# A hybrid decoder layer on one core: weights of every third MLP step combined on VectorE, one step in advance

## The chip, the cores and the metric

The kernel runs on one core of a Trainium2 chip. The core has a matrix engine (TensorE, called PE in the profile, with its weight loads as PEld), VectorE (DVE), ScalarE (ACT), GpSimd (POOL) and SyncE (SP), whose queue issues nearly all DMA transfers here. Each engine takes its instructions in order; engines wait for each other by semaphores. Tiles live in SBUF, a memory of 128 partitions; results of matmuls go to PSUM, eight banks of 128 x 512 float32.

The metric is the device time of one execution in microseconds (us), as a median over runs. A profile is one such execution with every instruction recorded.

## The reference, cut to what matters

One layer with 256 tokens and a width of 2048: a norm, one input projection, a state-space part and a sparse-attention part, an output projection into the residual, and then the MLP, which is the part that matters here:

```
u = rmsnorm(x, g_mlp) @ w_up                       # 256 x 2048 @ 2048 x 8192
return x + jnp.square(jax.nn.relu(u)) @ w_down     # 256 x 8192 @ 8192 x 2048
```

All is float32. The kernel reaches that precision by splitting each operand into a rounded part ("hi") and the rest ("lo"), both of a type that the matrix engine multiplies fast, and adding three products: hi x hi, lo x hi, hi x lo.

## The kernel before, in words

**Splitting weights.** Every weight goes the same way. SyncE's queue loads a block of 128 x 1024 float32 (512 KB) into a buffer called raw; ScalarE casts it to hi (line 144); VectorE subtracts hi from raw to get lo (line 145); hi and lo lie in one buffer, w2. There are RB = 4 raw buffers and WB = 5 w2 buffers. A raw buffer is free again when lo is made, a w2 buffer when the last matmul that reads it has run.

**The MLP.** The 8192 hidden columns are handled in pairs of 128-row blocks, 32 pairs, cut into three parts by `PARTS = (0, 11, 22, 32)`: 11, 11 and 10 pairs. For each part h, `up(h)` makes the hidden activations of all its pairs (line 230 holds the matmuls), and `down(h)` multiplies them with `w_down` and adds into the residual `xr`. The order on the profile's axis is up 0, down 0, up 1, down 1, up 2, down 2.

`down` runs over two halves j of the 2048 output columns. In each half it takes the pairs g in turn, a *step* each. A step has a 2 x 2 block of activations (two blocks of 128 tokens times two blocks of 128 hidden rows) and a 2 x 2 block of weights (two blocks of 128 hidden rows times two blocks of 512 columns). A plain step makes 8 products of blocks, each three matmuls of 512 columns in `three` (lines 189, 191, 192), so 24. The steps in `SEVEN = {2, 4, 6}` use seven products instead of eight (Winograd's form of Strassen's scheme), so 21 matmuls. For this, sums of the activations are made in `up` (lines 826 to 828), and sums of the weights in `weights` (lines 852 to 855): four subtractions of 128 x 512 on GpSimd, one after the other since three of them use the one before, one of them in place in raw. The results of the combination lie in raw[1] and in a tile t of 128 x 1536. Three casts (lines 860 and 863) and three subtractions (lines 861 and 864) split them into two w2 buffers and one buffer wt, of which there are two.

Four of the seven products are kept in accumulators of their own (p1, p5, p6, p7: four PSUM banks) over all three such steps of a half. After the last of these steps (`done`) they are combined on VectorE through two tiles s1 and s2 and added to the residual (lines 913 to 922). The other four banks hold the plain accumulators. The next half uses the two groups of four banks the other way round; so its plain products need the four banks of p1 to p7 from its first step on.

**What sets the order.** The matmuls run in the order in which the program states them. For the other engines and the DMA queues a planner orders the instructions at compile time by a model of their times: among those that are ready it takes the one with the highest priority, which is the order of the program, with all that stands under `tc.high_priority(offset=HP)` (loads and splits of weights) moved 600 instructions forward. On the chip each queue then keeps that order, and an instruction that has to wait holds up those behind it.

Of the kernel before, what the change touches and what calls it, by code (L numbers as in the profile page):

```python
# [9 lines left out]
F32 = mybir.dt.float32  # L10
# [3 lines left out]
OP = mybir.AluOpType  # L14
# [28 lines left out]
FIRST_W = 32  # L43


PARTS = (0, 11, 22, 32)
SEVEN = {2, 4, 6}

A11, A21, A12, A22 = range(4)
S3, S1, S2, S4 = 1, 4, 5, 6  # L50
# [34 lines left out]
def hymba_kernel(ctx: ExitStack, tc: tile.TileContext, xn, xt, w_in, w_out, w_up, w_down, vcol, vrow, out):  # L85
# [40 lines left out]
        return vc[:, VC[name] + i:VC[name] + i + 1]  # L126


    def operands(src, n, load=None, shift=0, parts=2):

        pitch = (n + 63) // 64 * 64
        with tc.high_priority(offset=HP):
            raw = wts.tile([P, parts, pitch], F32, name="raw", tag="raw", bufs=RB)
            both = wts.tile([P, 2 * parts * pitch + SPARE], F32R, name="w2", tag="w2", bufs=WB)
            hi, lo = (both[:, shift + i * parts * pitch:shift + (i + 1) * parts * pitch]
                      .rearrange("p (k c) -> p k c", k=parts)[:, :, :n] for i in range(2))
            src = src.rearrange("p (k c) -> p k c", k=parts)
            step = parts if load is None else 1
            for i in range(0, parts, step):
                s = slice(i, i + step)  # L140
                nc.sync.dma_start(raw[:, s, :n], src[:, s])
                if load is not None:
                    load()
                nc.scalar.copy(hi[:, s], raw[:, s, :n])  # L144
                nc.vector.tensor_tensor(lo[:, s], raw[:, s, :n], hi[:, s].bitcast(F32), op=OP.subtract)  # L145
        return hi, lo
# [663 lines left out]


    mlp = ctx.enter_context(tc.tile_pool(name="mlp", bufs=2))

    def up(h, tag):

# [18 lines left out]
            u.append((uh, ul))  # L834
        return u

    def weights(j, g, seven):


        if not seven:  # L840
            ops = [operands(w_down[2 * j + c, g], 512, shift=SHIFT) for c in range(2)]
            return [[(ops[c][0][:, k], ops[c][1][:, k]) for c in range(2)] for k in range(2)]
        with tc.high_priority(offset=HP):
            raws = []
            for c in range(2):
                raws.append(wts.tile([P, 2, 512], F32, name="raw", tag="raw", bufs=RB))
                nc.sync.dma_start(raws[c], w_down[2 * j + c, g].rearrange("p (k c) -> p k c", k=2))
            both = mlp.tile([P, 2 * 3 * 512 + SPARE], F32R, name="wt")
            th, tl = (both[:, SHIFT + i * 1536:SHIFT + (i + 1) * 1536].rearrange("p (k c) -> p k c", k=3) for i in range(2))
            t = mlp.tile([P, 3, 512], F32, name="t", bufs=1)  # L850

            nc.gpsimd.tensor_tensor(t[:, 0], raws[1][:, 1], raws[1][:, 0], op=OP.subtract)  # L852
            nc.gpsimd.tensor_tensor(raws[1][:, 0], raws[1][:, 0], raws[0][:, 0], op=OP.subtract)  # L853
            nc.gpsimd.tensor_tensor(t[:, 1], raws[1][:, 1], raws[1][:, 0], op=OP.subtract)  # L854
            nc.gpsimd.tensor_tensor(t[:, 2], raws[0][:, 1], t[:, 1], op=OP.subtract)  # L855
            ops = []
            for raw in raws:
                w2 = wts.tile([P, 2 * 2 * 512 + SPARE], F32R, name="w2", tag="w2", bufs=WB)
                hi, lo = (w2[:, SHIFT + i * 1024:SHIFT + (i + 1) * 1024].rearrange("p (k c) -> p k c", k=2) for i in range(2))
                nc.scalar.copy(hi, raw)  # L860
                nc.vector.tensor_tensor(lo, raw, hi.bitcast(F32), op=OP.subtract)  # L861
                ops.append((hi, lo))
            nc.scalar.copy(th, t)  # L863
            nc.vector.tensor_tensor(tl, t, th.bitcast(F32), op=OP.subtract)  # L864
        pick = lambda o, k: (o[0][:, k], o[1][:, k])
        (b11, b21), (t1, b22) = ([pick(o, k) for k in range(2)] for o in ops)
        t3, t2, t4 = (pick((th, tl), k) for k in range(3))
        return b11, b21, b22, t1, t2, t3, t4

    def down(h, u, tags):  # L870
        pairs = len(u)
        marked = SEVEN
        for j in range(2):
            end = h == 2 and j == 1
            outs = [accumulator(tags[j]) for _ in range(4)]
            acc = [outs[:2], outs[2:]]
            cut = CUTS if interrupted("down") else {}
            count = [0]

            def go(out, left, slot, w, first, last=False):  # L880
                three(out, left[0][:, slot], left[1][:, slot], *w, first, last, cut.get(count[0]))
                count[0] += 1

            def add(b, c, src, store=False):
                c = slice(1024 * j + c.start, 1024 * j + c.stop)
                nc.vector.scalar_tensor_tensor(xr[:, b, c], src, rs4[:, b:b + 1], xr[:, b, c], op0=OP.mult, op1=OP.add)
                if store:
                    nc.sync.dma_start(out[b * P:(b + 1) * P, c], xr[:, b, c])

            half = [slice(0, 512), slice(512, 1024)]  # L890
            ps7 = None
            kept = []
            for g in range(pairs):
                seven = g in marked
                w = weights(j, PARTS[h] + g, seven)
                if seven:
                    b11, b21, b22, t1, t2, t3, t4 = w
                    new = ps7 is None
                    if new:
                        ps7 = [accumulator(tags[1 - j]) for _ in range(4)]  # L900
                    p1, p5, p6, p7 = ps7
                    done = g == max(marked)
                    go(p1, u[g], A11, b11, new, done)
                    go(acc[0][0], u[g], A12, b21, False)
                    go(acc[0][1], u[g], S4, b22, False)
                    go(p5, u[g], S1, t1, new, done)
                    go(p7, u[g], S3, t3, new, done)
                    go(p6, u[g], S2, t2, new, done)
                    go(acc[1][0], u[g], A22, t4, False)
                    if done:  # L910

                        s1 = mlp.tile([P, 512], F32, name="s1", bufs=1)
                        nc.scalar.copy(s1, p1)
                        add(0, half[0], p1)
                        nc.vector.tensor_tensor(s1, s1, p6, op=OP.add)
                        s2 = mlp.tile([P, 512], F32, name="s2", bufs=1)
                        nc.vector.tensor_tensor(s2, s1, p7, op=OP.add)
                        add(1, half[0], s2)
                        nc.vector.tensor_tensor(s1, s1, p5, op=OP.add)
                        add(0, half[1], s1)  # L920
                        nc.vector.tensor_tensor(s2, s2, p5, op=OP.add)
                        add(1, half[1], s2)
                elif end and g >= pairs - 2:
                    kept.append((u[g], w))
                else:
                    for k in range(2):
                        for c in range(2):
                            for b in range(NB):
                                go(acc[b][c], u[g], 2 * k + b, w[k][c], g + k == 0, g == pairs - 1 and k == 1)
            if not end:  # L930
                for c in range(2):
                    for b in range(NB):
                        add(b, half[c], acc[b][c], h == 2)
                other.append("down")
                continue

            for b, c in ((0, 0), (1, 0), (0, 1)):
                for left, w in kept:
                    for k in range(2):
                        go(acc[b][c], left, 2 * k + b, w[k][c], False, left is u[-1] and k == 1)  # L940
                add(b, half[c], acc[b][c], True)
            c = slice(0, 256)
            for left, w in kept:
                for k in range(2):
                    go(acc[1][1][:, c], left, 2 * k + 1, [x[:, c] for x in w[k][1]], False, left is u[-1] and k == 1)
            add(1, slice(512, 768), acc[1][1][:, c], True)
            c = slice(256, 512)
            add(1, slice(768, 1024), acc[1][1][:, c])
            rest = accumulator(tags[0])[:, c]
            for i, (left, w) in enumerate(kept):  # L950
                for k in range(2):
                    go(rest, left, 2 * k + 1, [x[:, c] for x in w[k][1]], i + k == 0, left is u[-1] and k == 1)
            add(1, slice(768, 1024), rest, True)
# [56 lines left out]
```

## Time and profile before

| | |
|---|---|
| median of 3 runs | 1105.0 us (1101.55 to 1105.72) |
| the profiled execution | 1102.39 us, its span 1100.6 us |
| TensorE busy | 1070.3 us (97%) |
| VectorE, ScalarE, GpSimd busy | 746.4, 551.0, 123.5 us |
| mean granted clock of TensorE | 0.990 |
| bytes moved by DMA | 207.41 MB, mean 188 GB/s |

Rows of the profile name an engine, a line of the kernel, the tile written and, after the arrow, what was read (buffer numbers left out). In a row of waits, "A <- B: 15.6, 13, 1.3" says that A waited for B 15.6 us in all, in 13 places, 1.3 us at most. In a row of groups stand the count, the busy time, the mean duration in ns and the idle time before, with what ended it. In a table of stages each row has the stretch, its length, each engine's busy time with its number of instructions, the granted clock (1.00 is full speed), the DMA share and GB/s. Matmuls overlap in a pipeline: one of 512 columns is recorded with 0.38 us, while the next starts some 0.22 us after it.

### The profile page before, as it was taken

The numbers are of one execution on the slowest core, as the hardware profiler recorded it, in microseconds if no ns is written. First come the engines' busy times: TensorE is split into PE (matmuls) and PEld (weight loads), VectorE is DVE, ScalarE is ACT, GpSimd is POOL, SyncE is SP. The second block draws the span as 40 slices with busy tenths as digits, with TensorE's granted clock in tenths as the row PEclk, the third lists the DMA queues.
The fourth block names the chain that finished last, engine by engine and source line by source line (L and its number), as shares of the span: only waits on it lengthen the run. The fifth ranks groups of instructions, "written<-read, shape, count | busy, mean of one in ns | idle before, by whom it ended". The sixth has DMA issues, their size and how long they took to land.

```text
span 1100.6 us, 15648 instructions
## 1 busy us (share of the span) xinstructions
PE 1070.3 (97%) x5962; PEld 938.7 (85%) x5962; DVE 746.4 (68%) x1066; ACT 551.0 (50%) x749; POOL 123.5 (11%) x102
## 2 busy tenths in 40 slices
PE   9999999999999999999898999999998999998988
PEld 8999998888888898988686889897786888987876
DVE  6787997687665576764674767765665767754846
ACT  7755555567654554553544445544344445544433
POOL 0020000221000000003123000004123000023140
PEclk9999999999999999999999999999899999999999
DMA  9865437544565556664554766663554666645753
GB/s 329 261 213 182 158 105 241 172 135 135 165 236 187 187 185 201 196 197 150 186 178 161 242 207 195 194 207 134 192 186 169 226 202 192 198 147 172 239 163 115
DMA packets 63611, 207.41 MB, mean 188 GB/s; under 512 B 7088, under 2 KB 11440, under 8 KB 63536
## 3 DMA queue, kind: packets, MB, share of 16 engines
q1 hardware_dynamic: 63392, 206.36, 57.5%
q8 instruction: 47, 0.77, 0.3%
q14 instruction: 28, 0.23, 0.1%
q10 hardware_dynamic: 144, 0.05, 0.0%
HBM read 204.29 MB, written 2.10 MB: 188 GB/s over the span
## 4 chain that ended last, share of the span: by engine, by line
PE 73%; POOL 9%; DMA 5%; DVE 5%; issue 4%; ACT 4%; POOLq 0%; ACTq 0%; DVEq 0%
PE acc L230 29%; PE acc L192 10%; PE acc L209 10%; PE acc L189 10%; PE acc L191 10%; DMA raw<-in_w_down 5%; POOL raw L853 2%; DVE w L861 2%; POOL t L854 2%; POOL t L852 2%; POOL t L855 2%; ACT wt L863 2%; DVE w L145 2%; ACT w L144 2%; PE ps_y L610 1%
## 5 line engine op out<-in xcount | busy, mean ns | idle before, releaser
L145 DVE TENSOR_TENSOR w<-raw,w 128x1024 fp32r<-128x1024 f32 (+3 forms) x364 | 420.2, 1166 | 204.0 <-ACT w L144 203.1
L144 ACT CAST w<-raw 128x1024 fp32r<-128x1024 f32 (+3 forms) x364 | 357.5, 993 | 335.8 <-PE acc L192 104.7
L230 PE MATMUL acc<-x2x,w 128*128 128x512 f32 (+2 forms) x2053 | 343.0, 327 | 0.0
L230 PEld LDWEIGHTS acc<-x2x,w 128*128 128x128 f32 x2053 | 307.9, 188 | 34.4
L192 PE MATMUL acc<-w,uh 128*128 128x512 f32 (+1 forms) x444 | 171.9, 387 | 15.6 <-DVE w L861 15.6
L189 PE MATMUL acc<-w,uh 128*128 128x512 f32 (+5 forms) x459 | 171.4, 379 | 10.0 <-ACT w L860 10.0
L191 PE MATMUL acc<-w,ul 128*128 128x512 f32 (+1 forms) x444 | 169.4, 382 | 0.0
L209 PE MATMUL acc<-hx,w 128*128 128x256 f32 (+1 forms) x978 | 115.0, 277 | 0.0
L192 PEld LDWEIGHTS acc<-w,uh 128*128 128x128 f32 x444 | 83.7, 189 | 35.2 <-DVE w L861 21.0
L209 PEld LDWEIGHTS acc<-hx,w 128*128 128x128 f32 x978 | 112.7, 188 | 0.0
L189 PEld LDWEIGHTS acc<-w,uh 128*128 128x128 f32 x459 | 86.2, 188 | 29.2 <-ACT w L860 14.4
L864 DVE TENSOR_TENSOR wt<-t,wt 128x1536 fp32r<-128x1536 f32 x18 | 31.7, 1759 | 114.9 <-ACT wt L863 114.9
L852 POOL TENSOR_TENSOR t<-raw 128x512 f32<-128x512 f32 x18 | 24.7, 1373 | 716.5 <-DMA raw<-in_w_down 669.1
L191 PEld LDWEIGHTS acc<-w,ul 128*128 128x128 f32 x444 | 83.7, 188 | 14.4
L863 ACT CAST wt<-t 128x1536 fp32r<-128x1536 f32 x18 | 26.5, 1474 | 128.9 <-POOL t L855 128.9
L189 PE MATMUL acc<-w,hx 128*128 128x512 f32 (+3 forms) x228 | 83.9, 371 | 0.0
L191 PE MATMUL acc<-w,hx 128*128 128x512 f32 (+1 forms) x224 | 80.9, 361 | 0.0
L192 PE MATMUL acc<-w,hx 128*128 128x512 f32 (+1 forms) x224 | 80.7, 360 | 0.0
L189 PEld LDWEIGHTS acc<-w,hx 128*128 128x128 f32 x228 | 43.0, 189 | 6.1 <-issue 0.7
L191 PEld LDWEIGHTS acc<-w,hx 128*128 128x128 f32 x224 | 42.4, 189 | 5.9 <-issue 0.7
L192 PEld LDWEIGHTS acc<-w,hx 128*128 128x128 f32 x224 | 42.2, 189 | 6.0 <-DVE w L145 0.4
L861 DVE TENSOR_TENSOR w<-raw,w 128x1024 fp32r<-128x1024 f32 x36 | 46.1, 1279 | 0.2 <-ACT w L860 0.2
(229 smaller groups left out, 1033.3 us busy)
## 6 DMA issues: line engine op xcount, KB each, us to landing
raw<-in_w_up SPq DMA_DIRECT2D x128, 512.0 KB, 4.1
raw<-in_w_down SPq DMA_DIRECT2D x128, 512.0 KB, 4.3
raw<-in_w_in SPq DMA_DIRECT2D x72, 512.0 KB, 3.5
raw<-in_w_out SPq DMA_DIRECT2D x32, 512.0 KB, 3.3
raw<-in_w_in SPq DMA_DIRECT2D x16, 256.0 KB, 5.2
raw<-in_w_in SPq DMA_DIRECT2D x16, 152.0 KB, 5.2
raw<-in_w_in SPq DMA_DIRECT2D x8, 304.0 KB, 3.2
xT<-in_xt SPq DMA_DIRECT2D x8, 256.0 KB, 5.2
```

What stands on the lines that cost most here:

```text
L144: nc.scalar.copy(hi[:, s], raw[:, s, :n])
L145: nc.vector.tensor_tensor(lo[:, s], raw[:, s, :n], hi[:, s].bitcast(F32), op=OP.subtract)
L189: nc.tensor.matmul(go(out[:, i:j]), ah, go(wh[:, i:j]), start=first and i == 0, stop=False, skip_group_check=True)
L191: nc.tensor.matmul(go(out), al, go(wh), start=False, stop=False, skip_group_check=True)
L192: nc.tensor.matmul(go(out), ah, go(wl), start=False, stop=last, skip_group_check=True)
L209: nc.tensor.matmul(acc[:, c, at:at + n], w[:, 0, s], x[:, fr:fr + n], start=(i + k + j == 0), stop=(i >= 2 and k == 7 and j == len(todo) - ...
L230: nc.tensor.matmul(walk(out[:, at:at + n]), w[:, 0, s], walk(x[:, at:at + n]), start=(i < 2 and k + j == 0), stop=(i >= 2 and k == 7 and j ...
L852: nc.gpsimd.tensor_tensor(t[:, 0], raws[1][:, 1], raws[1][:, 0], op=OP.subtract)
L853: nc.gpsimd.tensor_tensor(raws[1][:, 0], raws[1][:, 0], raws[0][:, 0], op=OP.subtract)
L861: nc.vector.tensor_tensor(lo, raw, hi.bitcast(F32), op=OP.subtract)
L863: nc.scalar.copy(th, t)
L864: nc.vector.tensor_tensor(tl, t, th.bitcast(F32), op=OP.subtract)
```

## The change

- `PARTS` becomes (0, 10, 21, 32), so 10, 11 and 11 pairs, and `SEVEN` becomes {2, 5, 8}.
- While the MLP's pool exists, every second raw tile comes from it, under a tag with four buffers of its own: eight raw buffers from then on.
- `weights` is cut in three. `plain` is the old path of a plain step. `combine` loads the two raw tiles of a seven-product step and makes the four subtractions, now on VectorE; it is called one step earlier, ahead of the loads of the plain step before. `combined` makes the casts and rests, when the step itself comes.
- wt has one buffer instead of two, and s1 and s2 are taken from the two buffers of r (a tile that `up` uses) instead of having their own.

```diff
-PARTS = (0, 11, 22, 32)
-SEVEN = {2, 4, 6}
+PARTS = (0, 10, 21, 32)
+SEVEN = {2, 5, 8}
...
+    def raw_tile(parts, pitch):
+
+        taken[0] += 1
+        pool, tag = (mlp_pool[0], "rawm") if mlp_pool and taken[0] % 2 else (wts, "raw")
+        return pool.tile([P, parts, pitch], F32, name="raw", tag=tag, bufs=RB)
...
-            raw = wts.tile([P, parts, pitch], F32, name="raw", tag="raw", bufs=RB)
+            raw = raw_tile(parts, pitch)
...
+    def combine(j, g):
+
         with tc.high_priority(offset=HP):
             raws = []
             for c in range(2):
-                raws.append(wts.tile([P, 2, 512], F32, name="raw", tag="raw", bufs=RB))
+                raws.append(raw_tile(2, 512))
                 nc.sync.dma_start(raws[c], w_down[2 * j + c, g].rearrange("p (k c) -> p k c", k=2))
...
-            nc.gpsimd.tensor_tensor(t[:, 0], raws[1][:, 1], raws[1][:, 0], op=OP.subtract)
-            nc.gpsimd.tensor_tensor(raws[1][:, 0], raws[1][:, 0], raws[0][:, 0], op=OP.subtract)
-            nc.gpsimd.tensor_tensor(t[:, 1], raws[1][:, 1], raws[1][:, 0], op=OP.subtract)
-            nc.gpsimd.tensor_tensor(t[:, 2], raws[0][:, 1], t[:, 1], op=OP.subtract)
+            nc.vector.tensor_tensor(t[:, 0], raws[1][:, 1], raws[1][:, 0], op=OP.subtract)
+            nc.vector.tensor_tensor(raws[1][:, 0], raws[1][:, 0], raws[0][:, 0], op=OP.subtract)
+            nc.vector.tensor_tensor(t[:, 1], raws[1][:, 1], raws[1][:, 0], op=OP.subtract)
+            nc.vector.tensor_tensor(t[:, 2], raws[0][:, 1], t[:, 1], op=OP.subtract)
+        return raws[0], raws[1], t
+
+    def combined(raws):
+
+        ops = []
+        with tc.high_priority(offset=HP):
             for raw in raws:
-                w2 = wts.tile([P, 2 * 2 * 512 + SPARE], F32R, name="w2", tag="w2", bufs=WB)
...
+                n = raw.shape[1]
+                if n == 2:
+                    both = wts.tile([P, 2 * 2 * 512 + SPARE], F32R, name="w2", tag="w2", bufs=WB)
+                else:
+                    both = mlp.tile([P, 2 * 3 * 512 + SPARE], F32R, name="wt", bufs=1)
...
                 nc.scalar.copy(hi, raw)
                 nc.vector.tensor_tensor(lo, raw, hi.bitcast(F32), op=OP.subtract)
...
-                w = weights(j, PARTS[h] + g, seven)
+
+                if g + 1 in marked:
+                    ahead = combine(j, PARTS[h] + g + 1)
+                w = combined(ahead) if seven else plain(j, PARTS[h] + g)
...
-                        s1 = mlp.tile([P, 512], F32, name="s1", bufs=1)
+                        s1, s2 = (mlp.tile([P, 7, P], F32, name="r")[:, :4].rearrange("p k t -> p (k t)")
+                                  for _ in range(2))
...
-                        s2 = mlp.tile([P, 512], F32, name="s2", bufs=1)
```

More of the change, by code (lines that the diff above doesn't have):

```diff
@@ L126, in vcp @@
         return vc[:, VC[name] + i:VC[name] + i + 1]
+    mlp_pool = []
+    taken = [0]
+    def raw_tile(parts, pitch):
+        taken[0] += 1
+        pool, tag = (mlp_pool[0], "rawm") if mlp_pool and taken[0] % 2 else (wts, "raw")
+        return pool.tile([P, parts, pitch], F32, name="raw", tag=tag, bufs=RB)
     def operands(src, n, load=None, shift=0, parts=2):
@@ L812, in hymba_kernel @@
     mlp = ctx.enter_context(tc.tile_pool(name="mlp", bufs=2))
+    mlp_pool.append(mlp)
     def up(h, tag):
@@ L835, in up, with plain @@
         return u
[L837 to L842, printed above, removed]
+    def plain(j, g):
+        ops = [operands(w_down[2 * j + c, g], 512, shift=SHIFT) for c in range(2)]
+        return [[(ops[c][0][:, k], ops[c][1][:, k]) for c in range(2)] for k in range(2)]
+    def combine(j, g):
         with tc.high_priority(offset=HP):
@@ L845, in weights @@
             for c in range(2):
-                raws.append(wts.tile([P, 2, 512], F32, name="raw", tag="raw", bufs=RB))
+                raws.append(raw_tile(2, 512))
                 nc.sync.dma_start(raws[c], w_down[2 * j + c, g].rearrange("p (k c) -> p k c", k=2))
-            both = mlp.tile([P, 2 * 3 * 512 + SPARE], F32R, name="wt")
-            th, tl = (both[:, SHIFT + i * 1536:SHIFT + (i + 1) * 1536].rearrange("p (k c) -> p k c", k=3) for i in range(2))
             t = mlp.tile([P, 3, 512], F32, name="t", bufs=1)
-            nc.gpsimd.tensor_tensor(t[:, 0], raws[1][:, 1], raws[1][:, 0], op=OP.subtract)
@@ L853, in weights @@
[L853 to L856, printed above, removed]
-            for raw in raws:
-                w2 = wts.tile([P, 2 * 2 * 512 + SPARE], F32R, name="w2", tag="w2", bufs=WB)
-                hi, lo = (w2[:, SHIFT + i * 1024:SHIFT + (i + 1) * 1024].rearrange("p (k c) -> p k c", k=2) for i in range(2))
+            nc.vector.tensor_tensor(t[:, 0], raws[1][:, 1], raws[1][:, 0], op=OP.subtract)
@@ new lines, in combine @@
+            nc.vector.tensor_tensor(raws[1][:, 0], raws[1][:, 0], raws[0][:, 0], op=OP.subtract)
[5 more added lines that the diff above has]
+        with tc.high_priority(offset=HP):
+            for raw in raws:
+                n = raw.shape[1]
[3 more added lines that the diff above has]
+                    both = mlp.tile([P, 2 * 3 * 512 + SPARE], F32R, name="wt", bufs=1)
+                hi, lo = (both[:, SHIFT + i * n * 512:SHIFT + (i + 1) * n * 512].rearrange("p (k c) -> p k c", k=n)
+                          for i in range(2))
@@ L860, in weights @@
                 nc.scalar.copy(hi, raw)
                 nc.vector.tensor_tensor(lo, raw, hi.bitcast(F32), op=OP.subtract)
[L862 to L867, printed above, removed]
+                ops.append([(hi[:, k], lo[:, k]) for k in range(n)])
@@ L868, in weights @@
+        (b11, b21), (t1, b22), (t3, t2, t4) = ops
         return b11, b21, b22, t1, t2, t3, t4
```

## The prediction

> **What bounds the kernel now.** I read the page first, then the waits of the matrix engine, then busy time by stage, then the chain of waits. The page:
>
> ```profile
> span 1100.6 us, 15648 instructions
> PE 1070.3 (97%) x5962; PEld 938.7 (85%) x5962; DVE 746.4 (68%) x1066; ACT 551.0 (50%) x749; POOL 123.5 (11%) x102
> ```
>
> TensorE bounds the kernel: it is busy 1070.3 of 1100.6 us, and nothing off its path is worth anything. What it still waits for is this:
>
> ```profile
> PE acc L192 <- DVE w L861: 15.6, 13, 1.3
> PE acc L189 <- ACT w L860: 10.0, 8, 2.2
> PE ps_w L245 <- POOL ones L240: 1.3, 1, 1.3
> ```
>
> So 25.6 us in 21 waits, every one on lines 860 and 861, which split the weights of a step in seven products (below: a seven) into a rounded part and a rest. Plain steps are never waited for. By stage (us; PE, PEld, DVE, ACT, POOL busy; granted clock; DMA share; GB/s), the first three rows are the three down projections and the last two the up projections between them:
>
> ```profile
> 501.97:627.95 125.98, 117.37 (x518) 96.50 (x517) 78.92 (x76) 54.32 (x54) 32.50 (x24) 0.99 0.55 180
> 745.39:873.17 127.78, 119.85 (x517) 98.44 (x516) 78.98 (x77) 54.43 (x54) 31.80 (x23) 0.96 0.54 180
> 979.96:1097.12 117.16, 108.17 (x481) 89.08 (x479) 69.80 (x71) 45.93 (x46) 30.50 (x24) 0.97 0.49 165
> sum 370.92, PE 345.40 PEld 284.03 DVE 227.70 ACT 154.69 POOL 94.80; mean PE 115.13 PEld 94.68 DVE 75.90 ACT 51.56 POOL 31.60
> ...
> 627.95:745.39 117.44, 117.44 (x706) 105.67 (x705) 79.59 (x99) 57.96 (x75) 2.07 (x2) 1.00 0.63 202
> 873.17:979.96 106.79, 106.79 (x642) 96.07 (x641) 72.64 (x92) 52.71 (x68) 0.94 (x1) 1.00 0.62 198
> ```
>
> The up projections run without a gap at clock 1.00; nothing is to be had there. The down projections have gaps and a granted clock under 1. What they would take without both follows from their undisturbed pace, at the end of the first one (first and last of 108 matmuls of 512 columns, so 107 intervals):
>
> ```profile
> 603.77 0.38 PE L189 MATMUL acc<-w,uh 128*128 128x512 f32 x1
> ...
> 627.72 0.38 PE L192 MATMUL acc<-w,uh 128*128 128x512 f32 x1
> ```
>
> 23.95 / 107 = 0.2238 us each. A plain step has 24 such matmuls (5.37 us), a seven 21 (4.70 us). Each half of a stage of 11 pairs has 8 plain steps and 3 sevens, 255 matmuls; of 10 pairs, 231. So the stages need 2 x 255 x 0.2238 = 114.1, 114.1 and 103.4 us, 331.6 in all; they take 370.9. **39 us are lost**: 25.6 in waits, a few in emptying and refilling the pipeline 21 times, and the rest in the clock, which drops to half in five stretches:
>
> ```profile
> 590.95:594.37 3.42, 3.42 (x10) 2.64 (x9) 2.57 (x3) 0.03 (x1) 0.78 (x1) 0.50 0.89 277
> 782.10:788.93 6.83, 5.98 (x14) 4.72 (x15) 6.09 (x6) 3.39 (x5) 0.00 (x0) 0.50 0.64 212
> 846.95:850.37 3.42, 2.99 (x7) 2.41 (x8) 3.42 (x4) 1.71 (x3) 0.00 (x0) 0.50 0.50 166
> 1007.37:1010.79 3.42, 3.42 (x9) 2.67 (x8) 2.40 (x3) 0.00 (x0) 0.97 (x1) 0.50 0.86 275
> 1065.40:1068.82 3.42, 3.42 (x10) 2.65 (x9) 2.52 (x3) 0.00 (x0) 0.80 (x1) 0.50 0.89 268
> sum 20.51, PE 19.23 PEld 15.10 DVE 17.00 ACT 5.13 POOL 2.55; mean PE 3.85 PEld 3.02 DVE 3.40 ACT 1.03 POOL 0.51
> ```
>
> 20.5 us at clock 0.50 cost 10.3 us. Each stretch stands beside waits of a seven, and none lies in the 224 us of the up projections.
>
> Why sevens are late, in the chain of waits (start, us, what):
>
> ```profile
> 769.77 3.18 DMA raw<-in_w_down
> ...
> 773.12 1.26 POOL t L852
> ...
> 774.45 1.30 POOL raw L853
> ...
> 775.82 1.30 POOL t L854
> ...
> 777.19 1.29 POOL t L855
> ...
> 778.50 1.48 ACT wt L863
> ...
> 780.04 0.92 issue
> ...
> 781.68 1.23 DVE w L861
> ...
> 782.95 0.79 PE acc L192
> ```
>
> One loop is 13.2 us, 769.77 to 782.95: the load starts when a raw buffer is freed by the previous seven's split, then come four combinations on GpSimd, the casts, the rest on VectorE, which frees the buffer again. In that loop TensorE has one seven and one plain step, 10.1 us. It runs 3.1 us short each time, once the lead gained in plain steps is gone. SyncE's queue says which buffer is short:
>
> ```profile
> SPq L847 <- DVE w L861: 77.1, 24, 9.3
> SPq L847 <- POOL t L855: 43.2, 9, 6.2
> ```
>
> **The change part by part.**
>
> *Spacing.* Sevens stand at 2, 5, 8 instead of 2, 4, 6; their number (18) and that of the matmuls stay, so 331.6 us stay. From seven to seven TensorE now works 2 x 5.37 + 4.70 = 15.4 us. The same 13.2 us loop, unchanged otherwise, would already fit.
>
> *Eight raw buffers, loads ahead.* A seven's two loads are issued before the two of the plain step ahead of it, on the same SyncE queue, so that step's loads come two transfers later:
>
> ```profile
> raw<-in_w_down SPq DMA_DIRECT2D x128, 512.0 KB, 4.3
> ```
>
> Two landings one after the other, 8.6 us, is the most they can be late. Eight buffers are four steps, some 20 us, against two steps before; a buffer of a seven is reused four steps later. The DMA share stays near 0.55 to 0.63. Cost nothing while the loads lead by more than 8.6 us; if that cover is gone, the plain split is late next. The combination no longer starts behind a fresh load, which takes DMA out of the loop.
>
> *Combination on VectorE.* Four subtractions of 128x512 per seven. Rows of its durations:
>
> ```profile
> L145 DVE TENSOR_TENSOR w<-raw,w 128x1024 fp32r<-128x1024 f32 x173 | 210.1, 1232 | 89.3 <-ACT w L144 88.7
> L864 DVE TENSOR_TENSOR wt<-t,wt 128x1536 fp32r<-128x1536 f32 x18 | 31.7, 1759 | 114.9 <-ACT wt L863 114.9
> L833 DVE TENSOR_TENSOR ul<-r,uh 128x512 fp32r<-128x512 f32 x16 | 11.0, 686 | 0.0
> ```
>
> The same shape takes 686 ns: 2.7 us a seven, 49 us in 18. Half of a 1024-wide one (0.62) gives 44 us, the lower end; the upper end is GpSimd's own 1.3 us each, 94 us, which a VectorE of the same work does not come near, so I take 49. VectorE in the down projections then has 227.7 + 49 = 277 us against TensorE's 331.6, 84%, from 61%. It stays under the bound, so the work is hidden, but with little room. GpSimd's 94.8 us go. The casts of a seven on ScalarE now wait for VectorE; behind them queue the next plain casts, and behind those plain splits and TensorE. The 15.4 us between sevens cover that.
>
> *One buffer for the combined split (wt) instead of two.* Its cast and rest (1.48 and 1.76 us) must wait until the previous seven's last product, three steps earlier, is done, and then have two plain steps, 10.7 us. Nothing, with 7 us to spare; without it up to 3.2 us a seven. Behind that cast on ScalarE queue the next plain casts.
>
> *s1, s2 in the buffers of r.* Those are idle in a down projection and first written one product (10.7 us) into the next up projection: nothing.
>
> *The parts 10, 11, 11 and the last seven at 8.* Here something gets dearer. Behind the last seven, four sums are drained so that their PSUM banks can serve the next half. On VectorE, without interruption:
>
> ```profile
> 1027.47 0.68 DVE L915 TENSOR_TENSOR s<-s,acc 128x512 f32<-128x512 f32 x1
> ...
> 1030.18 0.68 DVE L921 TENSOR_TENSOR s<-s,acc 128x512 f32<-128x512 f32 x1
> ```
>
> 3.4 us, then 1.4 us more of adds that free no bank. Before, four plain steps (21 us) covered it. Now one does in the first part and two in the others: 5.37 + 0.67 + 1.34 = 7.4 us until the last bank is used (three matmuls before the seven's end, six into the next half), or 12.7. Weight splits go first in VectorE's order: in those 7.4 us may stand one or two 1.23, a 1.76 and a combination of 2.7, so 3.4 + 6 is up to 2 us late, with half-clock behind it up to 4. That is at two seams of the first part; at the other seams I see 0 to 1. Bounds 0 to 10 us, I take 5.
>
> A rule of the Trainium skill speaks to the clock. Page "TensorE: Matmul & The Clock Gate", section "HAM oscillation — how this bites in real kernels": only PE gaps longer than about 3.4 us bring the clock down. No run here shows a gap that long in these stages (the longest wait is 2.2 us), yet the clock falls next to them; by the rule the half-clock stretches would have another cause and stay, and the sum would end 10 us higher. I follow the trace, and count the other reading as a rival.
>
> **Sum.** The profiled execution took 1102.4 us, 1.8 around its span. 1102.4 - 39.3 = 1063.1, the floor; plus 5 at the seams = 1068. The median of the runs shown, 1105.0 (1101.55 to 1105.72), is 2.6 above the profiled one, so a median after may stand up to 2.6 higher: I say **1069**. Own range of this case 1062 to 1078.
>
> **The rivals.**
>
> 1. *VectorE becomes the limit in bursts.* It is in order; a wt rest, two raw rests and four combinations (1.76 + 2.46 + 2.7 = 6.9 us) may stand in front of a plain split. For it: 84% load. Against: five split buffers give TensorE at least one step and 1.3 us (6.7 us) of lead (the second buffer of a step was last used six matmuls before the end of the step two earlier), so a burst is barely uncovered. If half the waits stay, one of 1.1 us a seven: 1063 + 18 x 1.1 = 1083; range 1078 to 1092.
>
> 2. *The clock does not follow the waits* (the rule above as a mechanism here): the waits go, 20.5 us at half clock stay: 1068 + 10 = 1078. Against: all five stretches stand at sevens, none in the up projections.
>
> 3. *Another wait takes the old one's place, no change.* If the lead were set by the five split buffers and not by raw ones, casts would stay as late as now: 1100 to 1108. For it: casts wait for products often. Against: SyncE waits 120 us for sevens' raw buffers, and the loop above runs through them.
>
> 4. *Slower: the combination blocks VectorE's queue.* If the order puts it ahead of plain splits while its loads have not landed, then 4.3 (landing) + 2.7 + two splits of 1.23 = 9.5 us stand before a plain step's weights are ready, against 6.7 us of lead: 2.8 us lost a seven. It decides from 2.2 us a seven on (39.3 / 18). 18 x 2.8 = 50: 1063 + 50 = 1113. Against: with eight buffers the seven's slots were last used four steps before, so its loads should have landed.
>
> **How the numbers follow.** Forecast 0.68, rival 1 0.14, rival 2 0.04, rival 3 0.06, rival 4 0.08. Range 1061 to 1092: the forecast with rivals 1 and 2, 0.86 less a little at the edges. About 0.5% (5.5 us) is what a measurement can tell from no change: faster 0.86, same 0.06, slower 0.08.
>
> **What would show it.** Right: waits of PE on the split lines under 5 us in all, the down projections at 114 (two of them) and 104 us with granted clock 1.00, no GpSimd work in them, VectorE 84% there, SyncE no longer waiting for a seven's combination. Seams: a wait of the first matmuls of a half on lines 915 to 921 in the first part. Rival 1: waits on the rests with VectorE busy just before; rival 2: clock 0.50 without waits; rival 3: casts waiting for TensorE right before late splits; rival 4: VectorE idle, released by DMA of raw. Wrong altogether if sevens are waited for as now though their loads landed a step early.

## The result, and the profile after

The changed kernel takes 1072.6 us (median of 4 runs, 1071.39 to 1074.46) against 1104.4 before: a ratio of 0.9717, 95% interval 0.9692 to 0.9742. The forecast was 1069, range 1061 to 1092. The time was forecast well; as the experiments show, the reasons given for it were right only in part, and errors that cancel helped.

The page of the profile after (of the execution that took 1074.46 us), and below it all waits of TensorE:

```profile
span 1072.7 us, 15584 instructions
PE 1061.1 (99%) x5962; PEld 938.5 (87%) x5962; DVE 790.9 (74%) x1138; ACT 557.2 (52%) x749; POOL 25.1 (2%) x30
```

```profile
PE acc L198 <- DVE r L939: 4.4, 1, 4.4
PE acc L239 <- DVE x2x L707: 2.3, 2, 1.9
PE ps_w L254 <- POOL ones L249: 1.3, 1, 1.3
```

(New line numbers: 198 to 201 are the matmuls of a down projection, 239 those of an up projection, 861 to 864 the combination, 879 and 880 the cast and rest of a seven, 153 and 154 those of a plain step, 932 to 941 the drain of the four sums.) All 21 waits for a seven's weights are gone. One wait of 4.4 us at the drain of the sums and one in the first up projection are new. By stage, the same columns as in the prediction, up and down in turn:

```profile
383.60:495.93 112.33, 110.04 (x653) 98.49 (x651) 79.83 (x116) 57.15 (x77) 0.00 (x0) 0.98 0.62 206
495.93:605.78 109.85, 105.44 (x469) 88.75 (x468) 82.78 (x89) 50.72 (x49) 0.00 (x0) 0.97 0.57 192
605.78:726.35 120.57, 120.57 (x706) 106.61 (x705) 85.45 (x109) 59.29 (x76) 0.00 (x0) 1.00 0.59 192
726.35:838.87 112.52, 112.52 (x517) 96.16 (x516) 88.59 (x94) 54.88 (x53) 0.00 (x0) 1.00 0.63 204
838.87:956.33 117.46, 117.46 (x707) 105.76 (x705) 82.50 (x104) 59.47 (x76) 0.00 (x0) 1.00 0.61 199
956.33:1069.18 112.85, 112.85 (x529) 96.68 (x527) 87.67 (x95) 50.70 (x49) 0.00 (x0) 1.00 0.51 171
```

The down projections take 335.2 us instead of 370.9, 35.7 less. The second and third (rows 4 and 6) have no gap. Three rows are longer than they need be: the first up and first down projection, which hold the two new waits, and the second up projection, 120.57 us for the same 11 products that take 117.46 in the third, without any wait.

### The profile page after: what moved, and what is told of

It reads as the page before. It is cut to its first block, busy times and chain, and to the rows that moved or that the text cites. A ratio compares the mean times of both kernels' runs of the same rounds, so it can differ in the third digit from the quotient of the medians.

```text
span 1072.7 us, 15584 instructions
## 1 busy us (share of the span) xinstructions
PE 1061.1 (99%) x5962; PEld 938.5 (87%) x5962; DVE 790.9 (74%) x1138; ACT 557.2 (52%) x749; POOL 25.1 (2%) x30
## 4 chain that ended last, share of the span: by engine, by line
PE 96%; DMA 1%; DVE 1%; ACT 1%; issue 0%; SPq 0%; ACTq 0%; DVEq 0%
PE acc L239 32%; PE acc L198 17%; PE acc L200 17%; PE acc L201 17%; PE acc L218 10%; PE ps_y L619 1%; DVE w L154 1%; DMA raw<-in_w_down 1%; PE ps_l L657 0%; PE ps_o L682 0%; DMA xT<-in_xt 0%; PE ps_sr L703 0%; PE ps_s L509 0%; PE ps_s L510 0%; PE ps_dec L610 0%
## 5 line engine op out<-in xcount | busy, mean ns | idle before, releaser
L239 PE MATMUL acc<-x2x,w 128*128 128x512 f32 (+2 forms) x2053 | 348.2, 330 | 2.3 <-DVE x2x L707 2.3
L201 PE MATMUL acc<-w,uh 128*128 128x512 f32 (+1 forms) x444 | 169.2, 381 | 0.0
L879 ACT CAST w<-raw 128x1024 fp32r<-128x1024 f32 x36 | 37.7, 1047 | 53.4 <-PE acc L201 44.3
```

The lines of the kernel that those rows point to most:

```text
L201: nc.tensor.matmul(go(out), ah, go(wl), start=False, stop=last, skip_group_check=True)
L239: nc.tensor.matmul(walk(out[:, at:at + n]), w[:, 0, s], walk(x[:, at:at + n]), start=(i < 2 and k + j == 0), stop=(i >= 2 and k == 7 and j ...
```

## The experiments

Four edits are taken apart here: spacing (which also puts the drain shortly before the end of a half), eight raw buffers, combination on VectorE, and one step ahead. The single wt buffer, and s1 and s2 in r, only make room and were not tried by themselves. I began with the prediction's view, theory A (a seven's loop was longer than TensorE's work between two sevens, so the spacing matters most), against theory B (four raw buffers were the cause) and theory C (GpSimd was). Every ratio below is to the kernel before.

### Spacing alone

```diff
-PARTS = (0, 11, 22, 32)
-SEVEN = {2, 4, 6}
+PARTS = (0, 10, 21, 32)
+SEVEN = {2, 5, 8}
```

> The kernel before with nothing but the new parts (10, 11, 11) and the sevens at 2, 5, 8. Theory A (the loop of a seven was longer than TensorE's work between two sevens): the loop of 13.2 us now fits into 15.4 us, so nearly all waits on the split lines go by this alone: PE's waits on them under 6 us, time 1062 to 1074. Theory B (four raw buffers are the cause: a seven holds two of them for some 11 us whatever the spacing): the 18 waits stay, only spread: waits of 15 to 25 us, time 1085 to 1105.

1102.8 us, ratio 0.9989 (0.9960 to 1.0019): nothing. The waits are spread over more places and stay, 22.2 us on the split lines:

```profile
PE acc L192 <- DVE w L861: 16.9, 16, 1.3
PE acc L189 <- ACT w L860: 5.3, 9, 0.9
...
ACT wt L863 <- POOL t L855: 123.7, 18, 9.2
```

Theory A falls, and the time is where theory B had it. The last row points to the reason. It was in the profile before too, and the prediction had not used it; below it, two lines of ScalarE's timeline there (start, length, line, in brackets the idle time before):

```profile
ACT wt L863 <- POOL t L855: 128.9, 18, 8.1
```

```profile
778.50 1.47 ACT L863 CAST wt<-t 128x1536 fp32r<-128x1536 f32 x1 [7.89 <-POOL t L855]
779.88 1.04 ACT L860 CAST w<-raw 128x1024 fp32r<-128x1024 f32 x1
```

At the 18 sevens, ScalarE stood still for some 7 us each with the cast of the combined weights (wt) at the head of its queue, waiting for GpSimd. The second raw tile's cast, which TensorE needs before wt, stood behind it, and plain casts too. I read this as a delay within one seven, not a loop between two, so that more time between sevens doesn't cure it. The traces fit: GpSimd's first subtraction starts 11.1 us (median of 18) before TensorE's first matmul on wt in the kernel before, and 11.6 us with the new spacing. The wider spacing gave it no more lead.

### The old spacing with the rest of the change

```diff
-PARTS = (0, 10, 21, 32)
-SEVEN = {2, 5, 8}
+PARTS = (0, 11, 22, 32)
+SEVEN = {2, 4, 6}
```

> The changed kernel with the old parts (11, 11, 10) and the sevens at 2, 4, 6. Theory A (spacing): between two sevens TensorE has 10.1 us; VectorE then needs 2.5 for the plain splits, 4.2 for the seven's and 2.7 for the combination, 9.4 us, so it is nearly full and sevens are waited for again, by less than before: time 1070 to 1090. Theory B (buffers and loads ahead): waits on splits stay away, and with four plain steps behind the last seven the 4.4 us wait at the seam goes too: time 1058 to 1068.

1065.5 us, ratio 0.9683 (0.9640 to 0.9726). No wait in any down projection, the wait at the drain is gone too. These are theory B's numbers; the spacing isn't needed.

### The combination back on GpSimd, the rest of the change kept

```diff
-            nc.vector.tensor_tensor(t[:, 0], raws[1][:, 1], raws[1][:, 0], op=OP.subtract)
+            nc.gpsimd.tensor_tensor(t[:, 0], raws[1][:, 1], raws[1][:, 0], op=OP.subtract)
...
```

(The other three subtractions likewise.)

> The changed kernel with the four subtractions back on GpSimd. Theory A (spacing, and loads ahead): GpSimd's 5.2 us fit into 15.4 us, VectorE has 49 us less: no waits on splits, a smaller wait at the seam or none (no combination stands in front of the drain), time 1060 to 1072, not slower than the changed kernel. Theory C (GpSimd's slowness was the cause): waits on splits return, time over 1080.

1064.7 us, ratio 0.9652 (0.9623 to 0.9681): faster than the change itself, by an interval that doesn't touch its own. Theory C falls as the whole cause: with eight buffers and the loads ahead GpSimd is no hindrance, and without the combinations in VectorE's queue the drain isn't late.

### Four raw buffers, the rest of the change kept

```diff
-        pool, tag = (mlp_pool[0], "rawm") if mlp_pool and taken[0] % 2 else (wts, "raw")
+        pool, tag = wts, "raw"
```

> The changed kernel with four raw buffers instead of eight. Theory A (spacing): the loads of a seven start late again but the loop, now with 2.7 us of combination instead of 5.2, is some 10.5 us against 15.4: few waits, time 1065 to 1080. Theory B (buffers): a seven loaded a step ahead holds two of four buffers, the plain step between has two only; waits on plain splits appear, time 1085 or more. The 2.3 us wait in the first up projection (TensorE for x2x) should go if the extra loads made it.

1073.7 us, ratio 0.9743 (0.9712 to 0.9774): the same as the change. No wait on a seven. The wait at the drain grows to 6.5 us, that in the first up projection is gone. Theory B's 1085 or more is missed; the time lies in theory A's range, but theory A had fallen with the spacing. So neither eight buffers (here) nor VectorE (the run before) is indispensable; each seemed able to stand in for the other. That gave theory L: what a seven lacked was lead, from its load to its last split, and either one step ahead or more buffers gives it. Theory O: only the order in which loads are asked for counts.

### One step ahead, alone

```diff
-                w = weights(j, PARTS[h] + g, seven)
+                if g + 1 in marked:
+                    ahead = combine(j, PARTS[h] + g + 1)
+                w = combined(ahead) if seven else plain(j, PARTS[h] + g)
```

> The kernel before with one thing changed: the loads and the four subtractions of a seven (on GpSimd as before) are asked for one step earlier, ahead of the plain step's loads. Four raw buffers, sevens at 2, 4, 6, two wt buffers, s1 and s2 of their own. Theory L (lead: a seven needs 13 us from its load on, a plain step 6.6, and only the order of the loads gave both the same lead): waits on the split lines go, 1058 to 1068, below the changed kernel, as neither its seam nor its wait in the first up projection is there. Rival (the pieces work only together; four buffers with GpSimd's 5.2 us and 10.1 us between sevens are too few): 1075 to 1100.

1130.2 us, ratio 1.0239 (1.0186 to 1.0292): slower, and outside the ranges of both sides. TensorE now waits for plain steps, 42.6 us:

```profile
PE acc L198 <- ACT w L153: 26.9, 12, 3.5
PE acc L201 <- DVE w L154: 15.7, 14, 1.5
...
ACT wt L879 <- POOL t L864: 89.5, 18, 10.2
```

ScalarE's timeline of one such place shows a wt cast with the plain casts behind it:

```profile
519.27 1.47 ACT L879 CAST wt<-t 128x1536 fp32r<-128x1536 f32 x1 [6.85 <-POOL t L864]
520.64 1.99 ACT L153 CAST w<-raw 128x1024 fp32r<-128x1024 f32 x2
```

This is the fourth rival of the prediction, on ScalarE rather than VectorE: an instruction that waits, with other work behind it. Each of the 26 waits follows such a wt cast. But ScalarE also waits 68.6 us for loads of w_down by then, against 20.6 before, so late loads of plain steps (a seven loaded early holds two of the four buffers) have a share; the two were not separated. Theory L falls for "one step ahead".

### Eight raw buffers, alone

```diff
-            raw = wts.tile([P, parts, pitch], F32, name="raw", tag="raw", bufs=RB)
+            raw = raw_tile(parts, pitch)
...
-            both = mlp.tile([P, 2 * 3 * 512 + SPARE], F32R, name="wt")
+            both = mlp.tile([P, 2 * 3 * 512 + SPARE], F32R, name="wt", bufs=1)
```

(s1 and s2 in r, for room, as in the change.)

> Eight raw buffers (with one wt buffer, and s1 and s2 in r, to make room), but loads and GpSimd subtractions at the seven's own step, sevens at 2, 4, 6. Theory L (lead): eight buffers let the seven's load start two steps earlier even in the old order, so waits on splits go here too, 1060 to 1075. Theory O (only the order asked for counts, extra buffers are not used where they matter): waits of 15 to 25 us stay, 1085 to 1105.

1064.6 us, ratio 0.9639 (0.9600 to 0.9677). No wait in a down projection. One cure is found: eight buffers, with GpSimd, the old spacing and the old order of loads. ScalarE still waits for the combination, but less, and earlier than TensorE needs it: the first subtraction now starts 18.9 us (median) before TensorE's first matmul on wt.

```profile
ACT wt L879 <- POOL t L864: 47.3, 12, 6.2
```

### The change without the step ahead

```diff
-                if g + 1 in marked:
-                    ahead = combine(j, PARTS[h] + g + 1)
+                if seven:
+                    ahead = combine(j, PARTS[h] + g)
```

> The changed kernel with its loads and subtractions asked for at the seven's own step instead of one earlier. Theory L: eight buffers give the lead, and VectorE's shorter combination helps: no waits on splits but the seam, 1066 to 1076. Theory O: waits on splits return, 1085 or more.

1068.0 us, ratio 0.9669 (0.9629 to 0.9708). The wait at the drain is 2.3 us instead of 4.4. Asking a step earlier gains nothing here either; that it costs some 5 us is likely, but the two intervals overlap a little.

### The drain at the priority of the weight splits

```diff
+                        with tc.high_priority(offset=HP):
-                        nc.scalar.copy(s1, p1)
+                            nc.scalar.copy(s1, p1)
...
```

(All lines of the drain are indented under it.)

> The changed kernel with the drain of the four sums (lines 932 to 941) at the priority of the weight splits, so that it goes ahead of the splits and combinations of the next half. If the one wait of 4.4 us at the seam comes from what stands before the drain in VectorE's queue: it goes, with the half-clock behind it and the slower pace of the second up projection (0.2205 instead of 0.2245 us per matmul): 1060 to 1066. If it comes from the drain's own 3.4 us against one step of cover: it stays, 1070 to 1075.

1064.5 us, ratio 0.9652 (0.9594 to 0.9709). The 4.4 us wait is gone, and the second up projection takes 117.45 us. What had stood in front of the drain is in VectorE's timeline of the changed kernel:

```profile
545.49 0.75 DVE L901 SCALAR_TENSOR_TENSOR xr<-r,rs,xr 128x512 f32<-128x512 f32 x1
547.54 0.69 DVE L861 TENSOR_TENSOR t<-raw 128x512 f32<-128x512 f32 x1 [1.30 <-DMA raw<-in_w_down]
548.15 0.68 DVE L937 TENSOR_TENSOR r<-r,acc 128x512 f32<-128x512 f32 x1
548.75 1.22 DVE L154 TENSOR_TENSOR w<-raw,w 128x1024 fp32r<-128x1024 f32 x1
549.88 1.22 DVE L880 TENSOR_TENSOR w<-raw,w 128x1024 fp32r<-128x1024 f32 x1
551.02 0.69 DVE L862 TENSOR_TENSOR raw<-raw 128x512 f32<-128x512 f32 x1
551.62 0.74 DVE L901 SCALAR_TENSOR_TENSOR xr<-r,rs,xr 128x512 f32<-128x512 f32 x1
552.29 0.68 DVE L863 TENSOR_TENSOR t<-raw 128x512 f32<-128x512 f32 x1
552.89 0.68 DVE L939 TENSOR_TENSOR r<-r,acc 128x512 f32<-128x512 f32 x1
```

Line 939 frees the bank that TensorE waits for. From line 934 (542.51) to its end it takes 11.1 us instead of the 3.4 of the prediction: in between are a wt rest, two raw rests, three pieces of a later seven's combination, and 1.3 us in which VectorE waited for that combination's load.

### VectorE alone

Theory H: with four buffers what counts is how long a combination takes.

```diff
-            nc.gpsimd.tensor_tensor(t[:, 0], raws[1][:, 1], raws[1][:, 0], op=OP.subtract)
+            nc.vector.tensor_tensor(t[:, 0], raws[1][:, 1], raws[1][:, 0], op=OP.subtract)
...
```

(The four subtractions, and nothing else against the kernel before.)

> The kernel before with the four subtractions on VectorE instead of GpSimd and nothing else: four raw buffers, sevens at 2, 4, 6, loads in the old order. Theory H (four buffers hold a seven's load back, and what then counts is how long its buffers are held: 2.7 us of combination instead of 5.2 shortens the loop of 13.2 us to some 10.7 against TensorE's 10.1): small waits left, 1066 to 1085. Rival (with four buffers the load stays late, and the subtractions waiting for it now hold up VectorE's queue, the plain splits with it): 1090 to 1115.

1059.3 us (1058.76 to 1060.08), ratio 0.9605 (0.9579 to 0.9632): the second cure, better than forecast by either side, and 13 us faster than the whole change. Page, waits and the three down projections:

```profile
PE 1051.8 (100%) x5962; PEld 933.7 (88%) x5962; DVE 787.3 (74%) x1138; ACT 555.8 (53%) x749; POOL 25.2 (2%) x30
```

```profile
PE ps_w L245 <- POOL ones L240: 1.3, 1, 1.3
PE acc L189 <- ACT w L144: 0.3, 1, 0.3
...
ACT wt L863 <- DVE t L855: 18.3, 14, 1.5
```

```profile
501.96:614.46 112.50, 112.50 (x517) 96.12 (x516) 92.31 (x100) 55.76 (x54) 0.00 (x0) 1.00 0.61 204
731.91:844.43 112.52, 112.52 (x518) 96.13 (x516) 92.25 (x100) 55.88 (x54) 0.00 (x0) 1.00 0.62 203
951.21:1053.51 102.30, 102.30 (x481) 87.65 (x479) 85.23 (x95) 47.51 (x46) 0.00 (x0) 1.00 0.58 188
```

TensorE never waits in them, and the clock stays at 1.00. ScalarE's wait for the combined weights falls from 128.9 to 18.3 us.

### Eight raw buffers, the extra four from the first down projection on

```diff
-    mlp_pool.append(mlp)
...
-        down(h, up(h, tag), tags)
+        u = up(h, tag)
+        if not mlp_pool:
+            mlp_pool.append(mlp)
+        down(h, u, tags)
```

(Against eight raw buffers alone.)

> The kernel with eight raw buffers alone, its four extra ones in use only from the first down projection on. If the wait of some 2 us in the first up projection comes from three weight casts that the extra buffers put ahead of two casts of x2x in ScalarE's queue: it goes, with the half-clock behind it, some 3.5 us less than with eight buffers throughout: 1059 to 1062. If it has another cause: 1063 to 1066.

1060.0 us, ratio 0.9607 (0.9585 to 0.9630), 4.5 less than with eight throughout, and no wait in the first up projection. So that wait comes with the extra buffers. ScalarE's timeline in the changed kernel shows the three casts between casts of x2x (the MLP's input in the form that TensorE reads), for which TensorE waits:

```profile
388.63 0.47 ACT L706 ACTIVATE x2x<-ps_sr,vc 128x256 fp32r<-128x256 f32 x1 [1.06 <-DVE x2x L707]
389.27 2.95 ACT L153 CAST w<-raw 128x1024 fp32r<-128x1024 f32 x3 [0.17 <-DMA raw<-in_w_up]
392.12 0.46 ACT L706 ACTIVATE x2x<-ps_sr,vc 128x256 fp32r<-128x256 f32 x1
```

### Cut matmuls in every half

(A cut matmul is one of 512 columns that is issued as two.)

```diff
-            cut = CUTS if interrupted("down") else {}
+            interrupted("down")
+            cut = CUTS
```

> The changed kernel with the cut matmuls of the first step (five of them issued as two) in every half, not only in the first half of a stage. The wait at the seam falls in that step. If the slower pace behind it (0.2245 instead of 0.2205 us per matmul for 170 us) is a matter of how matmuls and weight loads fall against each other, some of the cuts come after the wait and the pace is 0.2205 again at once: 3 to 4 us less, 1067 to 1070. If it is the clock that stays lower after the wait: the pace stays 0.224, time 1071 to 1074.

1071.8 us (1069.24 to 1072.80), ratio 0.9713 (0.9687 to 0.9739): by time not to be told from the changed kernel, and in the range given for the clock. The trace says otherwise. The wait at the drain is still there (4.1 us, half-clock behind it), but the second up projection is back at 117.45 us:

```profile
606.61:724.06 117.45, 117.45 (x706) 105.69 (x705) 84.94 (x108) 59.47 (x76) 0.00 (x0) 1.00 0.61 197
```

### The wt cast behind both raw casts

The last run asks how much of the old loss was the order in ScalarE's queue (theory Q) and how much GpSimd's 5.2 us themselves (theory H).

```diff
-                nc.scalar.copy(hi, raw)
+                last = nc.scalar.copy(hi, raw)
...
-            nc.scalar.copy(th, t)
+            with tc.issue_after(last.ins):
+                nc.scalar.copy(th, t)
```

(Against the kernel before.)

> The kernel before with one change of order: the cast of the combined weights (wt) is queued on ScalarE behind both casts of the seven's raw tiles, where before it mostly stood ahead of the second, and its rest likewise on VectorE. GpSimd, four raw buffers, spacing and the order of loads stay. Theory Q (what costs is the wt cast, waiting at the head of ScalarE's queue for GpSimd with ready casts behind it): the second raw tile is split some 4 us earlier, its buffer is free and the next load starts earlier too, so most of the waits go: 1060 to 1075. Theory H (what costs is GpSimd's 5.2 us behind a late load, whatever the order): the waits move from the second raw tile to wt, which TensorE needs 2.7 us later: 1080 to 1100.

1080.2 us, ratio 0.9790 (0.9760 to 0.9820): at the lower edge of theory H's range, and about half of what VectorE alone gains. The waits that are left have moved to wt, as theory H has it, 11.0 us:

```profile
PE acc L192 <- DVE wt L865: 8.3, 9, 1.1
PE acc L189 <- ACT wt L864: 2.7, 3, 1.0
...
ACT w L860 <- POOL raw L853: 62.4, 15, 4.6
ACT wt L864 <- POOL t L855: 38.1, 15, 2.6
```

So both theories hold a part. This run gains some 22 us by the order; some 21 (1080.2 against 1059.3) are left, which VectorE gains too. The split isn't clean: in this run GpSimd's four subtractions take 7.2 us a seven instead of 5.5 before. Single ones take 2.15 us instead of 1.28 where VectorE's splits run beside them, so the new order seems to have made the combination itself slower.

## Why the prediction was right, and where it was not

**The bound and its size: right.** What was to be had were the waits on sevens and the half-clock behind them. With the waits gone, the clock is 1.00 in all three down projections of "VectorE alone". So the second rival (half-clock from another cause) falls, and with it, for this kernel, the rule of the Trainium skill that only gaps longer than about 3.4 us bring the clock down (page "TensorE: Matmul & The Clock Gate", section "HAM oscillation — how this bites in real kernels"; its words are "no PE-idle gaps >~3.4µs", the "only" is the prediction's): before, the clock fell beside waits of at most 2.2 us.

**The floor: 4 us too high.** It took 0.2238 us per matmul from the end of the first down projection. That stretch lay behind a wait and ran slow (last section). Undisturbed, the three down projections take 327.3 us, not 331.6. The floor is 1059, not 1063.

**Spacing ("the same 13.2 us loop would already fit"): the step that failed.** Spacing alone gives nothing (ratio 0.9989). I had read the chain of waits as a loop that has to turn once per pair of steps; it was a delay of each single seven, much of it spent at the head of ScalarE's queue. The row that says so, 128.9 us of ScalarE waiting for the combination, is among the longest in the list of waits, and the prediction argued from the rows of TensorE and SyncE alone. A seven's lead did not grow with the spacing (11.1 and 11.6 us); it grew with buffers (18.9 us).

**Eight raw buffers: right in effect, and enough alone.** They take away TensorE's waits with any of the other edits or none. The reason given, that the combination "no longer starts behind a fresh load", does not hold: in the changed kernel VectorE still waits for that load at 9 of the 18 combinations, 9.9 us in all, 1.3 of them at the drain. What counts is that it now happens early enough. What I costed at nothing was their effect elsewhere: in the first up projection they put casts in front of x2x, 2.3 us of waits, about 4 us in that stage.

**Combination on VectorE: cost right, use missed.** It adds 44.5 us to VectorE's busy time (746.4 to 790.9; forecast 49 with 44 as the lower end), hidden but for the drain. VectorE is busy 77% in the down projections of the change (259.0 of 335.2 us; forecast 84%), as part of the combinations has moved into up projections, and 82% in those of "VectorE alone" (269.8 of 327.3). But I put it down as a burden to be hidden. It is by itself a full cure; I take the reason to be that it ends sooner than GpSimd did. The first rival, VectorE as the limit, doesn't show except at the drain.

**One step ahead: costed at nothing, worth nothing or less.** With GpSimd and four buffers it costs 2.4%; in the change, the run without it is some 5 us faster, by intervals that overlap a little. There the combination starts some 24 us (median) before TensorE's first matmul on wt even without it, and 29 us with it.

**The drain: mechanism right, size too small.** Place (first part, where one step covers it), cause (splits and a combination first in VectorE's order) and line were as forecast. The wait of 4.4 us came at one of the two seams, with the half-clock behind it as said:

```profile
552.01:558.84 6.83, 5.22 (x12) 4.13 (x13) 4.80 (x8) 0.97 (x1) 0.00 (x0) 0.50 0.32 118
```

Not in the sum were 1.3 us of VectorE waiting for a load and the slow pace after it, 3.1 us in the second up projection. The first down projection, 109.9 us, is 7.6 above the 102.3 that 462 matmuls take undisturbed. All in all 11 us instead of 5, and 4 more in the first up projection. Floor 4 too high, extras 10 too low: that the time came out so near is in part luck, since errors cancel.

## What to carry to other kernels

Before an edit is credited with curing a wait, look at what every in-order queue on the way waits for, not only the bounding engine's: here a cast stood at the head of ScalarE's queue, waiting for GpSimd, with casts behind it that could have run. And take a change of several edits apart: four lines of this one gain 13 us more than all of it, since the other edits brought new waits of their own. Buffers added for one stage can re-order another through the planner, so look at the stages that weren't meant.

## What the runs showed of the hardware that I had not expected

After a wait, TensorE can run about 2% slower for a long time at a granted clock of 1.00. In the changed kernel the second up projection takes 120.57 us against 117.46 for the third, with the same 11 products and no gap in either. Start to start, its matmuls of 512 columns lie 0.225 us apart instead of 0.221 (medians over the trace's records). With cuts behind the wait, the same stage takes 117.45 us, though wait and half-clock remain. And in the run without the step ahead, no half-clock follows the wait of 2.3 us, yet the matmuls behind it, to the end of that stage, lie 0.2233 us apart on average, against 0.2200 ahead of it. So it isn't the granted clock. A cut can end it but does not always: a single one opens each up projection, and it ended the slow pace in the run without the step ahead (at 602.8 us) but not in the changed kernel (at 605.8 us). That it is the way in which matmuls and weight loads fall against each other is my reading, and no run shows that directly. It also spoiled the pace on which the prediction's floor rests.

What a wait costs in clock depends on where it falls. In all 14 profiles the granted clock changes only at whole multiples of 3.41 us from one another. Take the MLP's span in windows of this grid, and in each the time in which TensorE was idle by its records. Of the windows at full clock, all 25 with more than 1.77 us idle were followed by half clock, none of the 2756 with less than 1.63 us was, and of the 7 between, 3 were. So neither the longest wait nor the sum of two near ones decides. In the spacing run, gaps of 0.67 and 1.28 us made 1.85 us idle in one window (799.41 to 802.83 us) and brought half clock; two of 1.26 us each in the kernel before (at 524 and 526 us) lay in two windows and brought none. The 2.3 us at the drain of the run without the step ahead fell into two windows as well, 0.73 and 1.58 us, and brought none.
